# Weight tiles of the projections placed 64, 128 and 256 bytes past multiples of 2 KB in SBUF

## The chip, the cores and the metric

The kernel runs on one core of a Trainium2 chip. The metric is the device time of one execution in microseconds. The kernel before takes 1646.32 us, the median of three runs (1645.86 to 1648.91). All input and output is float32.

## The reference

One decoder layer over 1024 tokens of width 1024. The part that the change touches is the token mixer: one combined input projection of the normalised residual, two convolution branches, and their output projections.

```python
def token_mixer(h, w_in, conv_a_w, w_out_a, conv_b_w, conv_b_b, ln_b_g, ln_b_b, w_out_b, b_gate, w_o):
    proj = h @ w_in                                    # (1024 x 1024) @ (1024 x 7168)
    a_b, a_c, a_x, c_val, c_gate, gates = jnp.split(proj, cuts, axis=-1)
    y_a = (a_b * causal_dwconv(a_c * a_x, conv_a_w)) @ w_out_a
    u = c_val * jax.nn.sigmoid(c_gate)
    u = causal_dwconv(u, conv_b_w) + conv_b_b
    u = jax.nn.silu(layernorm(u, ln_b_g, ln_b_b))
    y_b = u @ w_out_b
    g = jax.nn.sigmoid(gates + b_gate)
    g_a, g_b = jnp.split(g, 2, axis=-1)
    return (g_a * y_a + g_b * y_b) @ w_o

def reference(...):
    h = rmsnorm(x, mix_norm_g[i])
    x = x + token_mixer(h, ...)
    h = rmsnorm(x, ffn_norm_g[i])
    x = x + hierarchical_moe(h, ...)      # top-1 of 4 groups, top-2 of its 8 experts
    hp = rmsnorm(x, ple_norm_g[i])
    x = x + jax.nn.sigmoid(hp @ w_ple_gate[i]) * (p[i] @ w_ple_proj[i])
    return rmsnorm(x, final_norm_g)
```

## The kernel before

**Products.** The projections keep float32 accuracy with three products of split operands in the type float32r: each operand is a high part (the value cast to float32r) and a low part (value minus high part), and a product is high by high, high by low and low by high. In a projection the weights are the stationary operand (128 x 128, loaded by a LDWEIGHTS of its own before each matmul) and the activations the moving one (128 x 512).

**A projection.** `proj` (L165) makes 128 output channels for all 1024 tokens. `wchunk` (L149) brings 128 columns of a weight matrix by one DMA on SP's queue into a raw tile (three buffers) and splits it: ScalarE writes the high part `wh` (L95), VectorE the low part `wl` (L96). `wh` and `wl` are rings of two buffers each in the pool `wring`. `proj_half` (L159) then issues, for one half of the tokens, 24 matmuls (L162): for each of 8 slices k of the contraction wh, wh, wl. So a projection is 48 matmuls, 32 of them with `wh` and 16 with `wl`. There are 72 projections: 56 column blocks of w_in, 8 of w_out_a and 8 of w_out_b, 3456 matmuls in all.

**Stages.** In stage s0 the rows are normalised, transposed and split into the tiles `a0` to `a7`; stage s1 (L227) makes five projections for each of 8 channel blocks, while VectorE runs the 31-tap convolution (L254); stage s2 (L314) makes the gates, both output projections and the layer norm. Then follow the product with w_o (L422), in which activations are stationary and the weights moving, the routing, the experts (L833, L860, plain float32 operands), and the last product with the gate weights (L1207 and L1274, again float32r, activations stationary). The instruction order of the first stages is set by the tile framework's scheduler, that of the later ones is written by hand.

**Addresses.** What matters here is where a tile begins in each partition of SBUF, modulo 2 KB. The pool of constants is padded (L134), so that the tiles `a0` to `a7` and `b0` to `b7`, of 8 KB each, begin at multiples of 2 KB; a moving operand is a run of 2 KB of such a tile, beginning at a multiple of 2 KB. In `wring` stand `vecs` (224 bytes), `cw` (1088) and a pad of 736, which make 2048 together; behind them lie the two buffers of `wh` and the two of `wl`, of 4096 bytes each. So all four begin at a multiple of 2 KB, and slice k of the weights at 512 k bytes behind one. The last product's operands and those of the product with w_o lie in the same way: the stationary ones at steps of 512 bytes from a multiple of 2 KB, the moving ones at a multiple of 2 KB (in L1274 some at 1 KB behind one). Behind `wring` lie the working tiles of the stages s1 and s2.

Of the kernel before, what the change touches and what calls it, by code (L numbers as in the profile page):

```python
# [10 lines left out]
F32 = mybir.dt.float32  # L11
F32R = mybir.dt.float32r
# [10 lines left out]
D = 1024  # L23
NT = 8
KT = 8
# [38 lines left out]
def layer_kernel(ctx: ExitStack, tc: tile.TileContext, A, out, dbg=None):  # L64
# [15 lines left out]
    def tpsum():  # L80
        return psum.tile([128, 512], F32, name="tp", bufs=2)
# [4 lines left out]
    def flat(t):  # L86
        return t.rearrange("p a b -> p (a b)")
# [6 lines left out]
    def split(h, l, src):  # L94
        nc.scalar.activation(h, src, AF.Copy)  # L95
        nc.vector.tensor_tensor(l, src, h.bitcast(F32), op=OP.subtract)  # L96

    def rstd_of(dst, ms):

        nc.gpsimd.tensor_scalar(dst, ms, EPS, None, op0=OP.add)  # L100
        nc.gpsimd.tensor_tensor(dst, dst, mhalf[:, :dst.shape[1]], op=OP.pow)
# [17 lines left out]
    def vec(i, k):  # L119
        return vecs[:, i * 8 + k:i * 8 + k + 1]  # L120
# [18 lines left out]
    wring = front.enter_context(tc.tile_pool(name="wring", bufs=2))  # L139
# [9 lines left out]
    def wchunk(src, c0, load_only=False):  # L149
        raw = wrawp.tile([128, KT, 128], F32, name="wraw")  # L150
        nc.sync.dma_start(raw, src[:, c0:c0 + 128].rearrange("(k p) n -> p k n", p=128))
        wh = wring.tile([128, KT, 128], F32R, name="wh")
        wl = wring.tile([128, KT, 128], F32R, name="wl")
        if load_only:
            return wh, wl, raw
        split(wh, wl, raw)
        return wh, wl
# [7 lines left out]
    def proj(src, c0, act):  # L165
        w = wchunk(src, c0)
        ps = mpsum()
        for hf in range(2):
            proj_half(w, ps, act, hf)
        return flat(ps)  # L170

    with tc.tile_pool(name="s0", bufs=1, side="right") as s0:
# [6 lines left out]
        for tb in range(NT):  # L179
            if tb == 4:  # L180
                first = [wchunk(w_in, (4 - i) * D, load_only=True) for i in range(2)]
            xt = s0.tile([128, D], F32, name=f"xt{tb}")
            nc.sync.dma_start(xt, A["x"][0, tb * 128:(tb + 1) * 128, :])
            xs.append(xt)
            for n, i, m in small[2 * tb:2 * tb + 2]:
                nc.sync.dma_start(vrow[i * 8:(i + m) * 8, :], A[n][0].rearrange("(k p) -> k p", p=128))
# [38 lines left out]


    with tc.tile_pool(name="s1", bufs=2) as s1:  # L227
        for cb in range(8):
            pg = proj(w_in, 4 * D + cb * 128, hT) if cb else flat(fps[0])
            sg = s1.tile([128, T], F32, name="tmp", bufs=2)  # L230
            nc.scalar.activation(sg, pg, AF.Sigmoid)
            pv = proj(w_in, 3 * D + cb * 128, hT) if cb else flat(fps[1])
            u = s1.tile([128, KB - 1 + T], F32, name="u")
            nc.gpsimd.memset(u[:, :KB - 1], 0.0)
            nc.vector.tensor_tensor(u[:, KB - 1:], pv, sg, op=OP.mult)
            acc = s1.tile([128, T], F32, name="acc")
            nc.scalar.activation(acc, u[:, :T], AF.Identity, scale=cw[:, cb, 0:1], bias=vec(V_CB, cb))  # L237
            pc = proj(w_in, D + cb * 128, hT)
            cx = s1.tile([128, T], F32, name="tmp", bufs=2)
            nc.scalar.activation(cx, pc, AF.Copy)  # L240
            px = proj(w_in, 2 * D + cb * 128, hT)
            m = s1.tile([128, 32 + T], F32, name="m", bufs=1)[:, :2 + T]
            nc.gpsimd.memset(m[:, :2], 0.0)
            nc.vector.tensor_tensor(m[:, 2:], px, cx, op=OP.mult)
            c3 = s1.tile([128, T], F32, name="c3", bufs=1)
            nc.scalar.activation(c3, m[:, :T], AF.Copy, scale=cw[:, cb, KB:KB + 1])
            for t in (1, 2):
                nc.vector.scalar_tensor_tensor(c3, m[:, t:t + T], cw[:, cb, KB + t:KB + t + 1], c3,
                                               op0=OP.mult, op1=OP.add)
            pb = proj(w_in, cb * 128, hT)  # L250
            nc.vector.tensor_tensor(c3, pb, c3, op=OP.mult)
            split(Y[0][cb], Y[1][cb], c3)
            for t in range(1, KB):
                nc.vector.scalar_tensor_tensor(acc, u[:, t:t + T], cw[:, cb, t:t + 1], acc,  # L254
                                               op0=OP.mult, op1=OP.add)
            nc.gpsimd.dma_start(u_dram[cb], acc)
# [57 lines left out]


    with tc.tile_pool(name="s2", bufs=2) as s2:
        def gate(c0, vi, ob):
            p = proj(w_in, c0 + ob * 128, hT)
            g = s2.tile([128, T], F32, name="g")
            nc.scalar.activation(g, p, AF.Sigmoid, bias=vec(vi, ob))  # L320
            return g

        def token_stat(acc, name):
            tp = tpsum()
            for tb in range(NT):
                nc.tensor.matmul(tp[:, tb:tb + 1], acc[:, tb * 128:(tb + 1) * 128], ones_col, start=True, stop=True)
            st = s2.tile([128, 32], F32, name=name, bufs=1)[:, :8]
            nc.vector.tensor_scalar(st, tp[:, :8], 1.0 / D, None, op0=OP.mult)
            return st

        def token_bcast(st, name):
            b = s2.tile([128, T], F32, name=name, bufs=1)
            for h in range(2):
                tp = tpsum()
                for j in range(4):
                    nc.tensor.transpose(tp[:, j * 128:(j + 1) * 128],
                                        st[:, h * 4 + j:h * 4 + j + 1].to_broadcast([128, 128]), ident)
                nc.scalar.activation(b[:, h * 512:(h + 1) * 512], tp, AF.Copy)
            return b

        def u_tile(cb):
            ut = s2.tile([128, T], F32, name="ut", bufs=2)
            nc.scalar.dma_start(ut, u_dram[cb])
            return ut

        def branch_a(ob):
            g = gate(5 * D, V_GA, ob)
            pa = proj(A["w_out_a"][0], ob * 128, Y)
            ma = s2.tile([128, T], F32, name="ma")
            nc.vector.tensor_tensor(ma, pa, g, op=OP.mult)  # L350
            nc.gpsimd.dma_start(mixa_dram[ob], ma)

        stat = s2.tile([128, T], F32, name="stat", bufs=1)
        for ob in range(4):
            branch_a(ob)
        for cb in range(0, 8):
            ut = u_tile(cb)
            if cb == 0:
                nc.scalar.activation(stat, ut, AF.Copy)
            else:  # L360
                nc.vector.tensor_tensor(stat, stat, ut, op=OP.add)
        mub = token_bcast(token_stat(stat, "mu"), "mub")
        for ob in range(4, 8):
            branch_a(ob)
        for cb in range(8):
            ut = u_tile(cb)
            nc.vector.tensor_tensor(ut, ut, mub, op=OP.subtract)
            if cb == 0:
                nc.scalar.activation(stat, ut, AF.Square)
            else:  # L370
                nc.scalar.activation(ut, ut, AF.Square)
                nc.vector.tensor_tensor(stat, stat, ut, op=OP.add)
        rs = token_stat(stat, "var")
        rstd_of(rs, rs)
        rsb = token_bcast(rs, "rsb")
        for ob in range(8):
            g = gate(6 * D, V_GB, ob)
            nc.gpsimd.dma_start(gb_dram[ob], g)
        S = Y
        for cb in range(8):  # L380
            ut = u_tile(cb)
            nc.vector.tensor_tensor(ut, ut, mub, op=OP.subtract)
            nc.vector.tensor_tensor(ut, ut, rsb, op=OP.mult)
            nc.scalar.activation(ut, ut, AF.Silu, scale=vec(V_LG, cb), bias=vec(V_LB, cb))
            split(S[0][cb], S[1][cb], ut)
        M = [a.rearrange("p (i k t) -> p i k t", i=2, k=KT) for a in bufA]
        for ob in range(8):
            pb = proj(A["w_out_b"][0], ob * 128, S)
            ma = s2.tile([128, T], F32, name="ma")
            nc.scalar.dma_start(ma, mixa_dram[ob])  # L390
            g = s2.tile([128, T], F32, name="g")
            nc.scalar.dma_start(g, gb_dram[ob])
            nc.vector.tensor_tensor(g, pb, g, op=OP.mult)
            nc.vector.tensor_tensor(ma, ma, g, op=OP.add)
            for tb in range(NT):
                split(M[tb][:, 0, ob], M[tb][:, 1, ob], ma[:, tb * 128:(tb + 1) * 128])
# [306 lines left out]
    n = []  # L703
# [611 lines left out]
```

## Time and profile before

| | |
|---|---|
| median of three runs | 1646.32 us |
| the profiled execution, its own time | 1647.99 us |
| its span, first to last instruction | 1646.2 us |
| mean granted TensorE clock, share of 2.4 GHz | 0.983 |
| TensorE matmuls busy | 1561.0 us, 95% |
| VectorE busy | 814.4 us, 49% |
| ScalarE busy | 351.3 us, 21% |
| matmuls of L162 | 3456 |

The profile gives for a matmul the time from its start to its modelled end, and matmuls overlap: the mean duration of one at L162 is some 390 ns, but the next starts long before that. The rate of a stream is read from the starts: the count in a stretch in which TensorE never rests, or the difference of two starts in the order of time. An instruction is counted in a window when any part of it lies in it.

### The profile page before, as it was taken

How to read it: one execution, taken by the hardware profiler on the slowest of the kernel's cores; microseconds unless marked ns; L12 is line 12 of the kernel's file. 1: busy time of each engine (PE TensorE's matmuls, PEld its weight loads, DVE VectorE, ACT ScalarE, POOL GpSimd, SP SyncE). 2: the span in 40 equal slices, each digit the busy share in tenths (PEclk: the TensorE clock that was granted, in tenths of full speed). 3: DMA queues.
4: the chain of work that ended last, by engine and by line, in shares of the span. 5: the costliest groups of instructions: out<-in, count | busy, mean ns of one | idle time of the engine just before them, and what ended most of it. 6: DMA issues, size and time to landing. Idle time of an engine off the chain costs nothing. (4 is left out here: it accounts for less than half of the span.)

```text
span 1646.2 us, 20527 instructions
## 1 busy us (share of the span) xinstructions
PE 1561.0 (95%) x8112; PEld 1068.9 (65%) x8112; DVE 814.4 (49%) x1113; ACT 351.3 (21%) x533; POOL 170.9 (10%) x318
## 2 busy tenths in 40 slices
PE   6999999999999999999999798999999999798898
PEld 4888888888888888888878642344444443343586
DVE  4899999999983432515554521111111212411575
ACT  4222212221121223632321210010100101010443
POOL 2300000000000001000022221111110101010131
PEclk9999999999999999999999988999999999899999
DMA  5221122212225333534365699999994989799741
GB/s 170 62 65 57 46 64 64 65 39 65 64 97 177 122 117 106 163 122 147 128 243 192 237 356 396 411 400 409 363 406 178 382 351 352 292 349 413 295 166 52
DMA packets 190669, 336.76 MB, mean 205 GB/s; under 512 B 10182, under 2 KB 85022, under 8 KB 190560
## 3 DMA queue, kind: packets, MB, share of 16 engines
q1 hardware_dynamic: 174080, 284.13, 47.5%
q0 software_dynamic: 10576, 29.96, 5.0%
q10 hardware_dynamic: 5904, 21.24, 4.0%
q8 instruction: 66, 1.08, 0.3%
q14 instruction: 43, 0.35, 0.1%
HBM read 302.67 MB, written 35.11 MB: 205 GB/s over the span
## 5 line engine op out<-in xcount | busy, mean ns | idle before, releaser
L162 PE MATMUL mm<-a,wh 128*128 128x512 f32 x1792 | 556.1, 391 | 0.9 <-ACT a L213 0.9
L162 PEld LDWEIGHTS mm<-a,wh 128*128 128x128 f32 x1792 | 336.9, 188 | 71.3 <-ACT a L213 1.5
L162 PE MATMUL mm<-a,wl 128*128 128x512 f32 x896 | 349.4, 390 | 0.0
L254 DVE SCALAR_TENSOR_TENSOR acc<-u,cw,acc 128x1024 f32<-128x1024 f32 x240 | 307.9, 1283 | 7.9 <-ACT acc L237 1.9
L162 PEld LDWEIGHTS mm<-a,wl 128*128 128x128 f32 x896 | 168.5, 188 | 34.4
L95 ACT ACTIVATE wh<-wraw 128x1024 fp32r<-128x1024 f32 x72 | 76.4, 1061 | 494.1 <-PE mm L162 422.7
L162 PE MATMUL mm<-b,wh 128*128 128x512 f32 x512 | 157.6, 389 | 0.0
L833 PE MATMUL p<-a,xts 128*32 128x256 f32 (+2 forms) x600 | 138.9, 520 | 8.4 <-DMA a<-in_w_exp_up_dram 5.1
L96 DVE TENSOR_TENSOR wl<-wraw,wh 128x1024 fp32r<-128x1024 f32 x72 | 87.7, 1218 | 72.9 <-ACT wh L95 72.8
L871 DVE COPY ys<-p 32x256 f32<-32x256 f32 (+2 forms) x60 | 31.3, 521 | 185.5 <-ACT ys L871 126.9
L833 PE MATMUL p<-b,xts 128*32 128x256 f32 (+2 forms) x528 | 109.6, 460 | 2.5 <-DMA b<-in_w_exp_up_dram 2.5
L162 PEld LDWEIGHTS mm<-b,wh 128*128 128x128 f32 x512 | 96.1, 188 | 19.9
L162 PE MATMUL mm<-b,wl 128*128 128x512 f32 x256 | 99.6, 389 | 0.0
L422 PE MATMUL mm<-b,a 128*128 128x512 f32 x384 | 95.8, 399 | 1.3 <-DVE b L96 1.3
L871 ACT COPY ys<-p 32x256 f32<-32x256 f32 (+2 forms) x60 | 26.6, 443 | 329.6 <-PE p L860 329.3
L833 PEld LDWEIGHTS p<-a,xts 128*32 128x32 f32 (+2 forms) x600 | 44.5, 136 | 78.7 <-issue 64.0
L838 DVE TENSOR_TENSOR hid<-p,hid 64x256 f32<-64x256 f32 (+2 forms) x41 | 22.7, 560 | 119.4 <-ACT hid L837 62.6
L422 PEld LDWEIGHTS mm<-b,a 128*128 128x128 f32 x384 | 69.6, 188 | 16.3 <-DVE b L96 2.1
L847 DVE COPY hT<-h 128x128 f32<-128x128 f32 (+2 forms) x41 | 17.3, 421 | 113.8 <-PE h L846 113.8
L833 PEld LDWEIGHTS p<-b,xts 128*32 128x32 f32 (+2 forms) x528 | 39.5, 133 | 43.6 <-issue 34.7
L699 POOL DMA_INDIRECT c<-h_dram,idx x39 | 37.8, 969 | 285.4 <-PE x L797 242.1
L860 PE MATMUL p<-a,hT 128*32 128x256 f32 (+2 forms) x440 | 67.4, 463 | 0.0
(322 smaller groups left out, 1551.2 us busy)
## 6 DMA issues: line engine op xcount, KB each, us to landing
a<-in_w_exp_down_dram SPq DMA_DIRECT2D x32, 1024.0 KB, 13.3
a<-in_w_exp_gate_dram SPq DMA_DIRECT2D x31, 1024.0 KB
b<-in_w_exp_up_dram SPq DMA_DIRECT2D x30, 1024.0 KB, 12.9
wraw<-in_w_in_dram SPq DMA_DIRECT2D x56, 512.0 KB, 3.6
b<-in_w_exp_down_dram SPq DMA_DIRECT2D x28, 1024.0 KB, 12.5
a<-in_w_exp_up_dram SPq DMA_DIRECT2D x27, 1024.0 KB, 13.1
b<-in_w_exp_gate_dram SPq DMA_DIRECT2D x24, 1024.0 KB
ut<-u_dram ACTq DMA_DIRECT2D x24, 512.0 KB, 4.6
```

What stands on the lines that cost most here:

```text
L95: nc.scalar.activation(h, src, AF.Copy)
L96: nc.vector.tensor_tensor(l, src, h.bitcast(F32), op=OP.subtract)
L162: nc.tensor.matmul(ps[:, hf], w[wi][:, k], act[ai][k][:, hf * 512:(hf + 1) * 512], start=(k == 0 and i == 0), stop=(k == KT - 1 and i == 2))
L254: nc.vector.scalar_tensor_tensor(acc, u[:, t:t + T], cw[:, cb, t:t + 1], acc, op0=OP.mult, op1=OP.add)
L422: nc.tensor.matmul(ps[-1][:, hf], act(a, k), w(b, k)[:, hf * 512:(hf + 1) * 512], start=(k == 0 and i == 0), stop=(k == nk - 1 and i == 2))
L699: return nc.gpsimd.indirect_dma_start(out=xg, out_offset=None, in_=h2_dram, in_offset=bass.IndirectOffsetOnAxis(ap=ix[:, 0:1], axis=0), bo ...
L833: nc.tensor.matmul(self.gu[j][p:p + r], self.x[:, k], w[:, i:i + self.gu[0].shape[1]], start=(k == 0), stop=(k == KT - 1))
L838: nc.vector.tensor_tensor(self.h, self.gu[1], self.h, op=OP.mult)
L847: nc.vector.tensor_copy(self.hT[:, :4], tp.rearrange("p (f t) -> p f t", f=4))
L860: nc.tensor.matmul(d, self.hT[:, f // 2 + f % 2 * 2 if r == 32 else f], w[:, c * n:(c + 1) * n], start=(f == 0), stop=(f == 3))
L871: (nc.scalar.copy if c < len(self.d) // 2 else nc.vector.tensor_copy)(self.y[:, c * n:(c + 1) * n], d)
```

## The change

The tile `wh` is made 16 elements (64 bytes) longer and `wl` 32 elements (128 bytes); the added elements are not used. With two buffers each, the four begin at 0 (`wh`, first buffer), 64 (`wh`, second), 128 (`wl`, first) and 256 bytes (`wl`, second) behind a multiple of 2 KB. These are 384 bytes more, and a pad of 1664 bytes at the head of s1 and of s2 makes them up to 2048: the working tiles of both stages move by exactly 2 KB and keep their places modulo 2 KB. All other tiles stay where they were. The instructions of every engine, their order, their shapes and what each waits for are the same as before; only addresses differ.

```diff
     def wchunk(src, c0, load_only=False):
         raw = wrawp.tile([128, KT, 128], F32, name="wraw")
         nc.sync.dma_start(raw, src[:, c0:c0 + 128].rearrange("(k p) n -> p k n", p=128))
-        wh = wring.tile([128, KT, 128], F32R, name="wh")
-        wl = wring.tile([128, KT, 128], F32R, name="wl")
+
+        wh = wring.tile([128, D + 16], F32R, name="wh")[:, :D].rearrange("p (k n) -> p k n", k=KT)
+        wl = wring.tile([128, D + 32], F32R, name="wl")[:, :D].rearrange("p (k n) -> p k n", k=KT)
         if load_only:
             return wh, wl, raw
         split(wh, wl, raw)
...
     with tc.tile_pool(name="s1", bufs=2) as s1:
+        s1.tile([128, 416], F32, name="pads", bufs=1)
...
     with tc.tile_pool(name="s2", bufs=2) as s2:
+        s2.tile([128, 416], F32, name="pads", bufs=1)
```

## Rows read from the trace of the kernel before

**Rows 1.** Four stretches of the projection stages: busy time of each engine in us, with the number of instructions in brackets, then the granted TensorE clock, the DMA share and GB/s.

```profile
200.00:400.00 200.00, 200.00 (x884) 165.63 (x883) 184.62 (x151) 38.75 (x37) 2.96 (x11) 1.00 0.20 61
400.00:500.00 100.00, 100.00 (x443) 82.80 (x442) 85.48 (x70) 20.50 (x20) 1.70 (x4) 1.00 0.27 85
620.00:700.00 80.00, 80.00 (x366) 66.39 (x365) 35.00 (x31) 41.58 (x39) 5.90 (x8) 1.00 0.43 138
700.00:800.00 100.00, 100.00 (x443) 82.83 (x442) 36.20 (x64) 28.32 (x58) 2.13 (x4) 1.00 0.41 132
```

The columns are: stretch, its length, PE, PEld, DVE, ACT, POOL, clock, DMA share, GB/s.

**Rows 2.** The page's costliest groups: the matmuls of the projections, the splits of their weights and the convolution. Columns: line, engine, operation, out<-in with shapes, count | busy us, mean ns of one | idle us before, and what ended it.

```profile
L162 PE MATMUL mm<-a,wh 128*128 128x512 f32 x1792 | 556.1, 391 | 0.9 <-ACT a L213 0.9
...
L162 PE MATMUL mm<-a,wl 128*128 128x512 f32 x896 | 349.4, 390 | 0.0
L254 DVE SCALAR_TENSOR_TENSOR acc<-u,cw,acc 128x1024 f32<-128x1024 f32 x240 | 307.9, 1283 | 7.9 <-ACT acc L237 1.9
...
L95 ACT ACTIVATE wh<-wraw 128x1024 fp32r<-128x1024 f32 x72 | 76.4, 1061 | 494.1 <-PE mm L162 422.7
L162 PE MATMUL mm<-b,wh 128*128 128x512 f32 x512 | 157.6, 389 | 0.0
...
L96 DVE TENSOR_TENSOR wl<-wraw,wh 128x1024 fp32r<-128x1024 f32 x72 | 87.7, 1218 | 72.9 <-ACT wh L95 72.8
...
L162 PE MATMUL mm<-b,wl 128*128 128x512 f32 x256 | 99.6, 389 | 0.0
```

**Rows 3.** The matmuls in order of time from 200 us, equal neighbours merged. Columns: start us, us from the first start to the last modelled end, engine, line, operation, out<-in, form, count.

```profile
199.87 0.39 PE L162 MATMUL mm<-a,wl 128*128 128x512 f32 x1
200.10 0.62 PE L162 MATMUL mm<-a,wh 128*128 128x512 f32 x2
200.55 0.39 PE L162 MATMUL mm<-a,wl 128*128 128x512 f32 x1
200.78 0.62 PE L162 MATMUL mm<-a,wh 128*128 128x512 f32 x2
201.23 0.39 PE L162 MATMUL mm<-a,wl 128*128 128x512 f32 x1
201.46 0.62 PE L162 MATMUL mm<-a,wh 128*128 128x512 f32 x2
201.91 0.39 PE L162 MATMUL mm<-a,wl 128*128 128x512 f32 x1
...
202.59 0.39 PE L162 MATMUL mm<-a,wl 128*128 128x512 f32 x1
...
203.27 0.39 PE L162 MATMUL mm<-a,wl 128*128 128x512 f32 x1
...
203.95 0.39 PE L162 MATMUL mm<-a,wl 128*128 128x512 f32 x1
...
204.63 0.39 PE L162 MATMUL mm<-a,wl 128*128 128x512 f32 x1
...
205.31 0.39 PE L162 MATMUL mm<-a,wl 128*128 128x512 f32 x1
```

**Rows 4.** The chain that ended last, in order of time, in the last product: start us, us, engine, what, line, count. The 48 at L1207 are 128 x 512; the 48 at L1274 are 24 of 128 x 512 and 24 of 128 x 256; the 24 of `h` at L1274 are 128 x 256.

```profile
1599.36 10.90 PE p L1207 x48
...
1627.01 8.31 PE p L1274 x48
1635.32 2.89 PE h L1274 x24
```

**Rows 5.** Matmuls of the experts in order of time, 128 x 512 on plain float32 operands, each with a weight load of its own; columns as in rows 3.

```profile
1250.15 13.90 PE L860 MATMUL p<-b,hT 128*128 128x512 f32 x32
```

**Rows 6.** Matmuls of the product with w_o right after two small matmuls of the routing have broken into the stream; columns as in rows 3.

```profile
903.08 0.28 PE L580 MATMUL tp<-payf,at 128*64 128x2 f32 x2
903.28 3.26 PE L422 MATMUL mm<-b,a 128*128 128x512 f32 x13
```

**Rows 7.** A weight load in the stream of rows 3, from the same view with TensorE's loads (PEld) in it; columns as there.

```profile
201.24 0.41 PEld L162 LDWEIGHTS mm<-a,wh 128*128 128x128 f32 x2
```

## The prediction

> **What bounds the kernel now.** I read the table of stretches first, because a change of addresses can only act where an engine reads or writes the moved tiles and these live in the stages s0 to s2. In four stretches of these TensorE is busy for the whole of each, 480 of 480 us, at a granted clock of 1.00, that is 2.4 GHz [rows 1]. Next the costliest groups: the 3456 matmuls of L162 stand in four groups, and TensorE sat idle 0.9 us before them in all [rows 2]. So these stages are as long as TensorE's matmuls follow each other, and nothing else sets their length. The splits that write the moved tiles are off the path: ScalarE's writes of wh wait 422.7 us in total for matmuls to give a buffer back, and VectorE's writes of wl wait for ScalarE [rows 2].
>
> **The rate of the stream.** From 200 to 400 us 884 matmuls are counted; one lasts 0.39 us and is counted from its start, so the window takes in starts over 200.39 us, and one follows the other by 200.39 / 884 = 226.7 ns [rows 1, 3]. At 2.4 GHz 512 columns take 213.3 ns, so each matmul has 13.4 ns that no column explains. Is it a fixed price or a share? The last product gives the answer with the same kind of operands: 48 of 512 columns in 10.90 us are 227.1 ns each, 24 of 256 columns in 2.89 us are 120.4 ns each, against 213.3 and 106.7 ns for the columns [rows 4]. The extra is 13.8 and 13.7 ns: a fixed price for each pair of weight load and matmul. Multiplied by the 3456 matmuls of L162 it is some 46 us of the kernel, and this is all that an address could give back.
>
> **The change part by part.** No instruction is added, removed or moved, and no wait. What remains are three terms.
>
> First, matmuls whose weights lie elsewhere. In a ring of two each buffer serves 36 of the 72 projections. The first buffer of wh stays at its place and with it 36 x 32 = 1152 matmuls. The second buffer of wh has 1152, the two of wl 576 each: 2304 matmuls get another offset between weights and moving operand. Their price at the new offset isn't in the trace, so I bound it. The lowest: the experts' matmuls of the same shape on plain float32 follow each other by (13.90 - 0.59) / 31 = 429 ns, with 0.59 us for the last one's duration, which is two passes of 214.7 ns [rows 5]; with the pair at that, 12.0 ns go, and 2304 x 12.0 = 27.6 us are won. The highest: after a break in the stream, 13 matmuls in the product with w_o take (3.26 - 0.39) / 12 = 239 ns each, the slowest unstalled run of that shape that I found, and this contains what the break itself cost [rows 6]; at that price 2304 x 12.5 = 28.8 us are lost.
>
> I take neither, but zero, for two reasons from rows. Slice k of the weights begins at 512 k bytes, so before the change the weight reads already begin at four different places modulo 2 KB, while the moving operand always begins at a multiple of 2 KB. If the meeting of equal places cost anything, slices 0 and 4 would be slower than 1, 2 and 3. The wl matmuls stand one per slice, and the differences of their starts are 0.68 us eight times in a row, 3 x 226.7 ns [rows 3]: all slices cost the same to within the 10 ns of the rows, about 3 ns for one matmul. And the reads do not stand still at their start: one weight read walks through 512 bytes, a moving read through 2 KB, in the same time. An offset of 64 to 256 bytes shifts when the two pass equal places, not how often they do. What these rows cannot exclude is an effect of the bits below 512 bytes at the start alone, because every start before is a multiple of 512. This is what keeps both ends in the range.
>
> The two-pass rows of the experts do not decide it. They have the same layout and almost no extra, but they take twice as long over the same bytes, so a collision could hide there.
>
> The fixed price is the same for all slices and in a product with quite other tiles [rows 3, 4]. The Trainium skill, in "TensorE: Matmul & The Clock Gate", section "Step-by-step: what each phase is for", says that TensorE has two independent read ports into SBUF, and that loading the next weights takes no read bandwidth from the running matmul. By that rule the sum of this term is 0 at any offset, as by the rows; 27.6 us would be won only if the rule failed.
>
> Second, the splits. ScalarE's write of wh takes 1.06 us and VectorE's subtraction 1.22 us, once per projection of 48 x 226.7 ns = 10.9 us [rows 2]. I know of no row that prices them at another offset; none is written across a different number of bytes. The cover: a channel block of s1 is five projections, 54.4 us, of which VectorE is busy 184.62 / 200, that is 50.2 us [rows 1]. The 4.2 us left are 0.84 us for each of five subtractions; they would have to grow from 1.22 to 2.06 us before TensorE waited. Value 0; each 0.1 us by which a subtraction grew beyond that would cost 40 x 0.1 = 4 us over the eight blocks. The cover holds in the other direction too: were 160 of the 240 matmuls of a block 12.0 ns faster, the block would be 52.5 us, still more than VectorE's 50.2.
>
> Third, the working tiles of s1 and s2, moved by 2 KB: their places modulo 2 KB are the same, and so are their waits. 0.
>
> Sum: 0 us. The profiled execution has a span of 1646.2 us and 1.8 us around it, 1647.99 us; it lies 1.7 us above the median of the runs, and since the sum is 0 the forecast is that median, 1646.3 us.
>
> **The rivals.** One: the reads do collide, and the offset resolves it. For it speaks that a fixed 13.7 ns stands beside each weight load [rows 4], and that a pass of 214.7 ns exists on this chip [rows 5]. Against it stand the equal slices [rows 3]. Its time is 1646.3 - 27.6 = 1618.7 us in full; where only some of the moved buffers gain, half of that, about 1632 us.
>
> A rule of the skill would make the same case: "TensorE: Matmul & The Clock Gate", section "Back-to-back issue gap", gives N / 2.4 + 2.5 ns, 215.8 ns for 512 columns. By it 10.9 ns of each matmul are to be had, an estimate of 25.1 us on 2304 matmuls, or 1621 us. The trace does not agree with that figure for these operands: it has 226.7 ns in steady state.
>
> Two, on the other side: the aligned start is the good one. The mechanism: the weight load of a wh pair starts at 201.24 us, the wl matmul that streams beside it at 201.23 us [rows 3, 7]: the two reads set out together, and with both at a multiple of 512 bytes the two reads may keep a fixed step that makes them miss each other, and a start 64 to 256 bytes off would break that step. For it speaks that the spacing is not one constant: after a break the same matmuls are slower for a while [rows 6]. Against it that the two reads cover unlike lengths in the same time. It decides from the first projection with a moved tile on; from 1.4 ns per moved matmul, 3.3 us in all, it shows as slower. Its price runs up to 28.8 us (1675 us); a mean of 3.5 ns, about a quarter of that end, gives 8 us, 1654 us.
>
> Three: the change doesn't do what it says. One third of the matmuls keep their offset, so whatever the offset does, only two thirds can show it; this is in the counts above and no case of its own.
>
> **How the numbers follow.** What can be told from no change is about 0.2%, 3.3 us. No effect: 0.68. Rival one: 0.17, of which 0.07 for the full gain and 0.10 for a part. Rival two, with the splits' case in it: 0.15. The range reaches from 1632 us, half of the full gain, to 1656 us, some 4 ns per moved matmul; what lies outside I put at 0.07 and a little below and 0.07 above. The case of no effect has a range of its own of 1643 to 1649.6 us.
>
> **What would show it.** Right: from 200 to 400 us again 884 matmuls, give or take two, wl starts 0.68 us apart in every projection, TensorE without idle time at L162, the writes at L95 and L96 at 1.06 and 1.22 us. Rival one shows as more matmuls in that stretch, up to 916 (two thirds at 214.7 ns and one third at 226.7, a mean of 218.7), with wl steps that differ from projection to projection as the buffers alternate. Rival two shows as fewer, 875 at a mean loss of 3.5 ns on two thirds. The prediction is wrong if the spacing in s1 differs between the two buffers, or if the time differs by over 3.3 us with the same spacing, which would mean a place that I did not name.

## The result and the profile after

The changed kernel takes 1662.14 us (median of four runs, 1658.54 to 1665.55) against 1647.54 us before (median of four): a ratio of 1.009 with a 95% interval of 1.0072 to 1.0109. It is slower by some 15 us; the forecast was no change, and its range ended at 1656 us.

The profiled execution has a span of 1663.8 us, 17.6 us more than before. The same stretches as in [rows 1], with the same columns:

```profile
200.00:400.00 200.00, 200.00 (x866) 162.97 (x865) 181.07 (x148) 38.03 (x36) 2.96 (x11) 1.00 0.19 58
400.00:500.00 100.00, 100.00 (x434) 81.44 (x433) 89.38 (x73) 18.06 (x17) 1.17 (x4) 1.00 0.21 66
620.00:700.00 80.00, 80.00 (x360) 65.36 (x359) 28.94 (x25) 35.83 (x33) 5.38 (x7) 1.00 0.38 120
700.00:800.00 100.00, 100.00 (x434) 81.50 (x433) 35.22 (x56) 32.62 (x56) 2.65 (x5) 1.00 0.42 136
```

TensorE is busy for the whole of each stretch and at full clock, as before. It only does less: 866 matmuls in the first 200 us and not 884, so one follows the other by 200.39 / 866 = 231.4 ns, where it was 226.7. VectorE's busy time falls with it (181.07 for 184.62 us), because it is fed more slowly.

How much of the loss is there? The view of one line gives the first and last start of its instructions. Of the kernel before, the first and last matmuls of the projections:

```profile
L162 PE MATMUL mm<-a,wh x1792: 387/389/796, 17.2 to 730.9; 128*128 128x512 f32 x200
...
L162 PE MATMUL mm<-b,wl x256: 388/389/390, 476.0 to 818.2; 128*128 128x512 f32 x128
```

and of the changed kernel (the line numbers are one higher):

```profile
L163 PE MATMUL mm<-a,wh x1792: 387/393/796, 17.8 to 745.2; 128*128 128x512 f32 x200
...
L163 PE MATMUL mm<-b,wl x256: 389/394/398, 485.4 to 834.2; 128*128 128x512 f32 x128
```

The projections last 834.2 - 17.8 = 816.4 us, before 818.2 - 17.2 = 801.0 us: 15.4 of the 17.6 us are in them, the whole size of the measured loss. The splits, which write the moved tiles, are as fast as in [rows 2], and the longer wait of ScalarE for TensorE is slack:

```profile
L95 ACT ACTIVATE wh<-wraw 128x1024 fp32r<-128x1024 f32 x72 | 76.4, 1061 | 515.8 <-PE mm L163 442.5
...
L96 DVE TENSOR_TENSOR wl<-wraw,wh 128x1024 fp32r<-128x1024 f32 x72 | 87.7, 1219 | 76.6 <-ACT wh L95 76.4
```

In order of time, the wl matmuls of one projection with the second buffers (wh at 64, wl at 256 bytes) and then of one with the first (wh at 0, wl at 128); columns as in [rows 3]:

```profile
200.93 0.39 PE L163 MATMUL mm<-a,wl 128*128 128x512 f32 x1
...
206.48 0.39 PE L163 MATMUL mm<-a,wl 128*128 128x512 f32 x1
...
208.56 0.40 PE L163 MATMUL mm<-a,wl 128*128 128x512 f32 x1
...
212.03 0.40 PE L163 MATMUL mm<-a,wl 128*128 128x512 f32 x1
```

Eight steps of three matmuls take 5.55 us with the second buffers and five take 3.47 us with the first: 694 ns for three in both, where [rows 3] has 680. So every projection is slower by the same 13 to 14 ns for three matmuls, although a third of the matmuls kept their weights' place.

Which of the three steps grew? The answer is worked out from the starts of projections 4 to 46 in the trace, from the fifth triple of each on. With the first buffers, the second wh matmul follows the first after 226.7 ns, as before; the wl matmul follows after 232.5 ns, and the next wh after 234.2. With the second buffers the steps are 225.8, 235.8 and 231.6 ns. So the loss sits at the steps into and out of the wl matmul, and the step between two wh matmuls costs nothing, even in the second buffers, where wh itself lies at 64 bytes.

### The profile page after: what moved, and what is told of

It is laid out like the page before. It is cut to its first block, busy times and chain, and to the rows that moved or that the text cites. A ratio compares the mean times of both kernels' runs of the same rounds, so it can differ in the third digit from the quotient of the medians.

```text
span 1663.8 us, 20527 instructions
## 1 busy us (share of the span) xinstructions
PE 1579.8 (95%) x8112; PEld 1072.5 (64%) x8112; DVE 815.0 (49%) x1113; ACT 351.4 (21%) x533; POOL 171.1 (10%) x318
## 5 line engine op out<-in xcount | busy, mean ns | idle before, releaser
L163 PE MATMUL mm<-a,wh 128*128 128x512 f32 x1792 | 562.6, 395 | 0.9 <-ACT a L214 0.9
L163 PE MATMUL mm<-a,wl 128*128 128x512 f32 x896 | 354.9, 396 | 0.0
L95 ACT ACTIVATE wh<-wraw 128x1024 fp32r<-128x1024 f32 x72 | 76.4, 1061 | 515.8 <-PE mm L163 442.5
L96 DVE TENSOR_TENSOR wl<-wraw,wh 128x1024 fp32r<-128x1024 f32 x72 | 87.7, 1219 | 76.6 <-ACT wh L95 76.4
L163 PEld LDWEIGHTS mm<-b,wh 128*128 128x128 f32 x512 | 96.4, 188 | 23.3
## 6 DMA issues: line engine op xcount, KB each, us to landing
a<-in_w_exp_down_dram SPq DMA_DIRECT2D x32, 1024.0 KB, 13.4
```

The lines of the kernel that those rows point to most:

```text
L163: nc.tensor.matmul(ps[:, hf], w[wi][:, k], act[ai][k][:, hf * 512:(hf + 1) * 512], start=(k == 0 and i == 0), stop=(k == KT - 1 and i == 2))
```

## The experiments

The unit below is the time of three successive matmuls of a projection (wh, wh, wl), 680 ns before; 72 projections have 1152 such triples. Three theories stood at first. A: a pair of load and matmul is dearer when the weights lie at another distance from the moving operand. B: what costs is that successive loads begin at different places, as wh and wl do. C: what costs is that the two buffers of a ring differ.

**All four tiles at 64 bytes.** The weight tiles get room to be placed by a function, on bases that are multiples of 1 KB; the other runs with `OFFSETS` (in elements of 4 bytes, for wh and wl of projection n) use the same lines.

```diff
+def OFFSETS(n):
+    return 16, 16
...
-        wh = wring.tile([128, KT, 128], F32R, name="wh")
-        wl = wring.tile([128, KT, 128], F32R, name="wl")
+        oh, ol = OFFSETS(turns[0])
+        turns[0] += 1
+        wh = wring.tile([128, D + 256], F32R, name="wh")[:, oh:oh + D].rearrange("p (k n) -> p k n", k=KT)
+        wl = wring.tile([128, D + 256], F32R, name="wl")[:, ol:ol + D].rearrange("p (k n) -> p k n", k=KT)
```

> All four weight tiles begin 64 bytes past a multiple of 512 bytes; the moving operand stays at multiples of 2 KB. Theory A (distance: a pair of load and matmul is dearer when the weights lie at another place than the moving operand): slower, since 64 bytes is one of the offsets of the changed kernel; three matmuls (wh, wh, wl) take about 693 ns as there, and the kernel about 1663 us. Theory B (change: what costs is that successive weight loads begin at different places modulo 512 bytes, as wh and wl do in the changed kernel; the distance to the moving operand costs nothing): no change, 680 ns for three matmuls, 1647 us.

1671.89 us, ratio 1.0146 (1.0113 to 1.0179). The first stretch, columns as in [rows 1]:

```profile
200.00:400.00 200.00, 200.00 (x859) 161.56 (x858) 179.42 (x146) 38.07 (x36) 2.95 (x11) 1.00 0.19 58
```

200.39 / 859 = 233.3 ns for one, 700 ns for three: dearer than the changed kernel, with all four tiles alike. B and C fall as the whole cause, A stands, with a larger price than it had named (20 and not 13 ns; 1152 x 20 = 23.0 us, measured 23.3). Here all three steps are 233.3 ns, the one between two wh matmuls too.

**The low part alone at 128 bytes.**

```diff
+def OFFSETS(n):
+    return 0, 32
```

> One part of the change alone: both buffers of wl begin 128 bytes past a multiple of 512 bytes, both of wh at a multiple. Theory A: only the wl matmuls can pay, in all projections; if 128 bytes cost what they cost in the changed kernel's first buffers, 693 ns for three matmuls, about 1663 us. Theory B: wh and wl differ in every projection, so the full price although only a third of the matmuls have moved: 693 ns for three, about 1663 us. Theory C (what costs is that the two buffers of a ring lie at different places, so that one projection differs from the next): no change, 680 ns and 1647 us.

1663.15 us, ratio 1.0095 (1.0061 to 1.0129), with 867 matmuls in the first stretch:

```profile
200.00:400.00 200.00, 200.00 (x867) 163.82 (x866) 181.16 (x148) 38.06 (x36) 2.96 (x11) 1.00 0.20 60
```

231.1 ns for one, 693 for three: one matmul in three has moved, and the loss is that of the whole change. C falls again. From the starts, the step into the wl matmul is 232.5 ns, the one out of it, to a wh that has not moved, 234.2, and the one between two wh matmuls 226.7.

**Two maps.** Each projection has a pair of its own. In the first map the 35 pairs follow each other and come again in reverse order.

```diff
+BYTES = (
+    (0, 0), (16, 16), (32, 32), (64, 64), (128, 128), (256, 256), (448, 448),
+    (0, 16), (0, 32), (0, 48), (0, 64), (0, 96), (0, 128), (0, 192),
+    (0, 256), (0, 320), (0, 384), (0, 448), (0, 480), (16, 0), (32, 0),
+    (64, 0), (128, 0), (256, 0), (384, 0), (64, 128), (64, 192), (128, 64),
+    (256, 128), (128, 256), (64, 256), (0, 512), (0, 1024), (512, 0), (0, 544),
+)
+def OFFSETS(n):
+    if n < 2:
+        return 0, 0
+    oh, ol = BYTES[n - 2 if n < 37 else 71 - n]
+    return oh // 4, ol // 4
```

> A map: each of 70 projections has its own pair of offsets for wh and wl (35 pairs, each twice, the second time in reverse order). Read is what three matmuls (wh, wh, wl) take within a projection. Theory A: pairs of equal offsets (16 to 448 bytes) are as dear as (0, same offset), about 693 ns; (0, 0) 680 ns. Theory B: equal offsets 680 ns at any offset; unequal ones about 693 ns, and the same for (0, o) as for (o, 0); differences of 512 and 1024 bytes 680 ns, (0, 544) as (0, 32). Either theory leaves open whether the price grows with the difference or steps up at some size; a flat one would be 693 ns from 16 to 480 bytes.

In the second every pair is entered from a projection at (0, 0), and `BYTES` is another list of 35 pairs.

```diff
+def OFFSETS(n):
+    if n < 3 or n % 2 == 0:
+        return 0, 0
+    oh, ol = BYTES[(n - 3) // 2]
+    return oh // 4, ol // 4
```

> A second map, in which every second projection has both weight tiles at 0, so that each pair of offsets is met from the same state. If the distance modulo 256 bytes decides: (256, 256), (512, 512) 680 ns for three matmuls; (272, 272) as (16, 16), (320, 320) as (64, 64), (32, 288) as (32, 32), (64, 320) as (64, 64), (128, 384) as (128, 128). The pairs with 16 bytes or less, entered from 680 ns, are expected at 680 ns; if one stands below 680 ns, the price of 13 ns that the kernel before pays at each pair of load and matmul can be lowered by an address, and otherwise it can't by this means.

The reading is the step from one wl matmul to the next. Four projections of the second map, ten steps apart each: (32, 32), then (0, 0), then (256, 256), then (320, 320).

```profile
173.56 0.40 PE L182 MATMUL mm<-a,wl 128*128 128x512 f32 x1
...
180.56 0.40 PE L182 MATMUL mm<-a,wl 128*128 128x512 f32 x1
...
182.63 0.39 PE L182 MATMUL mm<-a,wl 128*128 128x512 f32 x1
...
189.44 0.39 PE L182 MATMUL mm<-a,wl 128*128 128x512 f32 x1
...
591.37 0.39 PE L182 MATMUL mm<-b,wl 128*128 128x512 f32 x1
...
598.17 0.39 PE L182 MATMUL mm<-b,wl 128*128 128x512 f32 x1
...
635.63 0.40 PE L182 MATMUL mm<-b,wl 128*128 128x512 f32 x1
...
642.63 0.40 PE L182 MATMUL mm<-b,wl 128*128 128x512 f32 x1
```

These are 700, 681, 680 and 700 ns a step. The table has the same reading of most of the pairs, as the mean of a projection's sixteen triples, worked out from all the starts in the two traces (two values: both maps' or both passes' readings):

```
wh and wl both at o bytes:   4: 697   8: 692   12: 680   16: 680 or 700   24: 693   32: 700
                            48: 700  64: 700   96: 703  128: 697  160: 700  192: 687  224: 700
                           240: 680 248: 700  252: 680  256: 680  272: 680  320: 700  512: 680
wl alone (0, o):            16: 680, 696  32: 699, 700  64: 693, 693  128: 694, 693  192: 693, 693
                           256: 680, 681 384: 694, 695 448: 693, 693  512: 680  544: 699  1024: 680
wh alone (o, 0):            16: 680 to 699  32: 696, 696  64: 700, 700  128: 700, 700
                           256: 680 (683 where other matmuls broke in)  384: 700, 701  512: 681
```

Three things follow. First, the price repeats with 256 bytes: (320, 320) is (64, 64), (0, 544) is (0, 32), and multiples of 256 cost nothing. Theory A holds in this form. It does not hold as a price that each matmul pays by its own distance: wl alone at 64 bytes makes 693 ns, wh alone 700, and both together 700. Nor was either expectation met in full: A had equal offsets as dear as one tile moved alone, and the second map had the pairs at 4 and 8 bytes at 680 ns, where they stand at 692 to 700. Second, nothing is below 680 ns: of the offsets tried none gives back the 13.4 ns that each pair pays before the change. Third, at 16 bytes the outcome depends on what came before. In the first map (16, 16) stands once behind (0, 0) and once behind (32, 32):

```profile
62.44 0.39 PE L182 MATMUL mm<-a,wl 128*128 128x512 f32 x1
...
69.24 0.39 PE L182 MATMUL mm<-a,wl 128*128 128x512 f32 x1
...
810.55 0.40 PE L182 MATMUL mm<-b,wl 128*128 128x512 f32 x1
...
817.55 0.40 PE L182 MATMUL mm<-b,wl 128*128 128x512 f32 x1
```

6.80 us for ten steps the first time and 7.00 us the second, from the same offsets. These two differ in the ring's buffer and in the moving tile as well. A pair that doesn't is (16, 0), in the second buffers and with the moving tiles `a` both times, in the first map behind (0, 480) and in the second behind (0, 0):

```profile
260.99 0.39 PE L182 MATMUL mm<-a,wl 128*128 128x512 f32 x1
...
267.99 0.39 PE L182 MATMUL mm<-a,wl 128*128 128x512 f32 x1
...
434.65 0.39 PE L182 MATMUL mm<-a,wl 128*128 128x512 f32 x1
...
441.45 0.39 PE L182 MATMUL mm<-a,wl 128*128 128x512 f32 x1
```

Again 7.00 and 6.80 us. The changed kernel's own second pair, (64, 256), does it too: it takes 694 ns there, entered from (0, 128), and 700 ns both times in the first map, the second time entered from (0, 512):

```profile
482.29 0.40 PE L182 MATMUL mm<-b,wl 128*128 128x512 f32 x1
...
489.29 0.40 PE L182 MATMUL mm<-b,wl 128*128 128x512 f32 x1
```

So it is no fixed charge on an address, and the map's entry for a pair is a reading from one state. The offsets 12, 240 and 252 were met only once alike for both tiles, from the fast state. In the changed kernel the starts show that after a few triples the three steps repeat to the end of a projection (with the second buffers 226, 236 and 232 ns). It looks as if the two reads of TensorE fell into one pattern or another and stayed in it, which the runs suggest and don't show.

**The order of the products.** On the changed kernel's addresses:

```diff
-            for i, (wi, ai) in enumerate(((0, 0), (0, 1), (1, 0))):
+            for i, (wi, ai) in enumerate(PASSES[::-1] if k % 2 else PASSES):
```

> The changed kernel's addresses, but every second slice of the contraction takes its three products in reverse order (wl, wh, wh after wh, wh, wl), so that wl loads stand in pairs and the change between wh and wl happens twice in six matmuls and not four times. Theory A: the same pairs of addresses, so the same price, 693 ns for three and about 1662 us. Theory B: half the changes, half the price: about 687 ns for three and 1655 us.

1667.12 us, ratio 1.0119 (1.0085 to 1.0152), 862 matmuls in the first stretch, 697 ns for three. Fewer changes between wh and wl made it dearer, not cheaper, which is against B; and the steps between two equal tiles, wh and wh or wl and wl, are slow here as well, 231 to 235 ns from the starts. It isn't A's unchanged 693 either; the price depends on the order in which the offsets follow each other.

**Which of the two operands.** Theory A leaves open whether the distance counts (R), the weights' own place (W), or the place of each operand (V). First everything behind the constants is moved by 64 bytes:

```diff
-    const.tile([128, 104], F32, name="pad")
+    const.tile([128, 120], F32, name="pad")
```

> The pad of the constants is 64 bytes longer, so that the moving operands, the weight tiles and all tiles behind them move by 64 bytes together; the distance between weights and moving operand is that of the kernel before. Theory R (what counts is the distance from the start of the moving operand to that of the weights, modulo 256 bytes): no change, 680 ns for three matmuls, 1647 us. Theory W (the weights themselves must begin at multiples of 256 bytes, the moving operand may lie anywhere): slow, as with the weights alone at 64 bytes, 700 ns and about 1671 us. Theory V (each of the two operands must begin at such a multiple): slow too, 700 ns or more.

Then the moving operand without the weight tiles (the raw tiles that are split go with it), by the same line and

```diff
-    wring.tile([128, 184], F32, name="padw", bufs=1)
+    wring.tile([128, 168], F32, name="padw", bufs=1)
```

> The moving operands begin 64 bytes past a multiple of 2 KB, the weight tiles at a multiple of 2 KB as before. Theory R: slow, about 695 to 700 ns for three matmuls, since the distance is now 192 modulo 256; 1665 to 1671 us. Theory W: no change, 680 ns and 1647 us. Theory V: slow. R and V are told apart by the kernel with everything moved together.

The first stretch with everything moved:

```profile
200.00:400.00 200.00, 200.00 (x884) 165.62 (x883) 184.67 (x151) 39.12 (x37) 2.97 (x11) 1.00 0.19 60
```

and with the moving operand moved against the weight tiles:

```profile
200.00:400.00 200.00, 200.00 (x875) 164.09 (x875) 182.80 (x148) 38.02 (x36) 2.97 (x11) 1.00 0.20 61
```

884 matmuls, 680 ns for three: weights at 64 bytes cost nothing when the moving operand lies there too, so W and V fall. 875 matmuls, 687 ns: the weight tiles haven't moved and the rate falls, to the very 687 ns that the map has for a distance of 192 bytes (0 - 64 is 192 modulo 256). R holds; that run's expectation of 695 to 700 ns was a guess ahead of that entry of the map. The times of the whole kernels, 1658.23 us (ratio 1.0058, 1.0036 to 1.0079) and 1666.53 us (1.0107, 1.0078 to 1.0137), are some 10 us above what the projections explain; the last section takes that up.

**A stagger in steps of 256 bytes.**

```diff
+def OFFSETS(n):
+    return ((0, 128), (64, 192))[n % 2]
```

> The weight tiles are staggered as in the changed kernel, each buffer at a place of its own, but in steps of 256 bytes (0 and 512, 256 and 768 past a multiple of 1 KB) and not of 64 and 128. If a stagger as such cost something, about 1662 us; if only distances that are no multiple of 256 bytes do, no change: 680 ns for three matmuls and 1647 us.

1650.09 us, ratio 1.0006 (0.9992 to 1.0020), and the first stretch as before the change:

```profile
200.00:400.00 200.00, 200.00 (x884) 165.60 (x883) 184.67 (x150) 38.38 (x37) 2.97 (x11) 1.00 0.20 61
```

A stagger as such is harmless; this one also moves the tiles of s1 and s2 by 4 KB, and nothing came of that.

**A forecast from the map.** One line of the kernel before is moved to another place:

```diff
-    wring.tile([128, 184], F32, name="padw", bufs=1)
...
     with tc.tile_pool(name="s1", bufs=2) as s1:
+        s1.tile([128, 184], F32, name="pads", bufs=1)
...
     with tc.tile_pool(name="s2", bufs=2) as s2:
+        s2.tile([128, 184], F32, name="pads", bufs=1)
```

> The pad of 736 bytes ahead of the weight tiles is taken out and put ahead of the working tiles of s1 and s2: all four weight tiles begin 1312 bytes past a multiple of 2 KB, which is 32 modulo 256, and the moving operand at 0. By the two maps the pair (32, 32) takes 699.5 ns for three matmuls, 19.5 ns more than 680; 1152 such triples make 22.5 us, so 1670.5 us. If what counts were a stagger of the four tiles among themselves, they have none here: 1648 us.

1670.51 us, ratio 1.0154 (1.0132 to 1.0176), with 858 matmuls in the first stretch:

```profile
200.00:400.00 200.00, 200.00 (x858) 160.99 (x858) 179.41 (x146) 38.10 (x36) 2.96 (x11) 1.00 0.19 58
```

The map's entry for (32, 32) gives the time of the whole kernel: 23.6 us lost, where the entry makes 22.5; that the total agrees to 0.01 us is luck. The run also shows what the pad of 736 bytes is worth in the kernel before: some 23 us.

No run beat the kernel before: its weights already lie at the cheapest distance that was found.

## Why the prediction was wrong

**What bounds the kernel.** Right: TensorE sets the length of these stages, busy for the whole of the four stretches in both kernels, and 15.4 of the 17.6 us were lost there.

**The fixed price.** Its size was right (13.4 ns beside the columns), and so was the use made of [rows 4]. Of "all that an address could give back", no offset tried gave back anything.

**The first term** is the step that failed: it was set at 0 and is 15.4 us. Both reasons given for zero were wrong. The first, that slices at 512 k bytes all cost the same [rows 3], rested on rows that could not speak: 0, 512, 1024 and 1536 are all 0 modulo 256, so the four places were one place. The prediction said itself that bits below 512 were open, and then gave that too little weight. The second, "an offset of 64 to 256 bytes shifts when the two pass equal places, not how often they do", is refuted by the maps: the rate changes with the offset. Its premise, that the two reads take the same time, isn't in the rows either: 165.63 us for 883 loads are 188 ns for one [rows 1], and the matmuls follow each other after 226.7. The bounds held: the dearest whole kernel lost 23.6 us (1670.51 against 1646.94 us), within the 28.8 us taken from [rows 6].

**Whom it touches.** The count of 2304 moved matmuls was wrong as a measure, and so was "only two thirds can show it". Every projection slows alike, and within it the steps into and out of the wl matmul: with wl alone moved, the wh matmul behind it is late too (234.2 ns), and in the changed kernel the wh matmuls that moved are on time among themselves (225.8 ns). So the price isn't that of the moved weights alone; it depends on what follows what in the stream. The prediction's own signs of being wrong, a spacing that differs between the buffers or another time at the same spacing, left out what came: another spacing, the same in both.

**The rule on the two reads.** Weighed in the prediction, the Trainium skill ("TensorE: Matmul & The Clock Gate", section "Step-by-step: what each phase is for") has loading the next weights take nothing from the running matmul. These runs do not agree: with everything else equal the matmul rate follows the distance between the starts of the two operands, 226.7 to 233.3 ns. The Trainium skill's formula for the gap (same page, section "Back-to-back issue gap"), 215.8 ns for 512 columns, stands there for an isolated matmul and not, as the prediction used it, for a stream of pairs of load and matmul; it was reached at no offset tried.

**The splits and the working tiles.** Right: 1061 and 1219 ns, no cover was needed, and the working tiles, moved by 2 KB here and by 4 KB in the run with steps of 256 bytes, cost nothing that shows.

**Rival two** had the sign and the place, and of its mechanism the first half: equal starts are the good ones. That the reads set out together and keep a step is not shown, and its bounds were wrong: a start 256 bytes off, which it counted among the bad ones, costs nothing, and starts that are all 64 bytes off cost nothing either. It was mis-sized: 3.5 ns on 2304 matmuls, 8 us, against 15.4 / 3456 = 4.5 ns on all of them. Its own range reached the result; the chance of 0.15 for it was too small, and the range of the whole ended 6 us too early. Its sign in the trace was the one that it named, fewer matmuls in the stretch (866; it said 875).

**Rival one** fell: no offset tried made a projection faster. Its pass of 214.7 ns was half of the 429 ns of [rows 5]; that these are two passes is shown by no run.

What stays open is what in the memory has the period of 256 bytes, why some distances (12, 240, 252) cost nothing and their neighbours do, what puts the stream into one pattern or the other, and whether the slow matmuls after a break [rows 6] are the same effect. No run tried these.

## What to carry to other kernels

In a stream of float32r matmuls that each load their weights, keep the distance between the start of the weights and the start of the moving operand at a multiple of 256 bytes, for every weight tile in the stream; a stray tile of a few hundred bytes ahead of either cost some 3% of the stream's rate here (233.3 ns for 226.7). When a trace shows no difference between several addresses, look first at what they have in common: equal costs at 0, 512, 1024 and 1536 say nothing of 64. A map with one setting per loop turn gives dozens of such readings from one execution; enter each setting from more than one neighbour, since the one before can decide the reading.

## What the runs showed of the hardware

That the rate of a matmul stream depends on the distance of its two operands modulo 256 bytes, and that the stream can stay fast or slow at the same offsets (680 or 700 ns for three matmuls at (16, 0)), was not expected.

Nor was the loss of the kernel whose tiles had all moved by 64 bytes. Its projections ran at 680 ns, so it was lost elsewhere. The experts' stage, from the first of its transposes to the last of its matmuls, before and with everything moved by 64 bytes (columns as in [rows 1]):

```profile
947.40:1526.00 578.60, 535.98 (x3430) 227.74 (x3434) 115.90 (x230) 55.49 (x115) 76.03 (x82) 0.97 0.95 362
```

```profile
944.50:1530.00 585.50, 540.58 (x3430) 228.01 (x3434) 115.87 (x230) 55.59 (x115) 76.23 (x82) 0.96 0.97 358
```

It takes 6.9 us longer, with the DMA engines busier (0.97 for 0.95) and moving less (358 for 362 GB/s). Not all of that is the tiles: the stage of the kernel with steps of 256 bytes, whose target tiles had not moved, and that of the kernel with the moving operand at 64 bytes, whose target tiles had, are

```profile
948.00:1529.00 581.00, 540.66 (x3434) 228.69 (x3434) 115.87 (x230) 55.59 (x115) 76.22 (x82) 0.96 0.95 361
```

```profile
954.70:1540.00 585.30, 539.08 (x3432) 228.74 (x3434) 115.87 (x230) 55.59 (x115) 76.22 (x82) 0.96 0.97 357
```

Measured in all twelve traces, the stage lasts 579 to 581 us in the ten with the tiles `a` and `b` at multiples of 256 bytes and some 586 us in the two with them at 64. The same tiles moved by 256 bytes tell whether that goes:

```diff
-    const.tile([128, 104], F32, name="pad")
+    const.tile([128, 168], F32, name="pad")
```

> As the run that moved everything by 64 bytes, but by 256. That run had its projections at 680 ns for three matmuls and yet lost some 10 us, 7 of them in the experts' stage, where the DMA queues brought at most 398 GB/s in a slice and not 413. Theory F (the transfers into tiles that begin 64 bytes off are slower): at 256 bytes this goes, if 256 suffices as a boundary; 680 ns, 1648 us, slices of 413 GB/s again. Theory G (it is the distance between these tiles and the constants, which stay where they are, or to the ends of memory): still about 1657 us.

1648.79 us, ratio 1.0014 (0.9999 to 1.0028): it goes. The GB/s line of the page's 40 slices, for 64 bytes and then for 256:

```profile
GB/s 170 62 65 64 39 64 64 65 50 53 64 120 162 115 115 129 141 126 153 133 259 183 237 360 381 394 384 391 388 388 209 364 364 350 300 345 397 298 166 52
```

```profile
GB/s 170 62 63 54 51 64 64 64 40 64 64 93 177 120 122 101 168 119 146 132 244 191 237 359 397 410 401 396 354 406 178 379 370 352 294 346 413 293 166 52
```

The fastest slice has 397 GB/s with tiles 64 bytes off and 413 GB/s at 256, as theory F has it. In a stage whose DMA engines are busy for 0.95 of the time, an offset of 64 bytes in the target tiles was worth 4 to 7 us in the profiled executions. Of everything moved by 64 bytes that execution, at 1652.28 us, was the fastest of its kernel's runs; where the other runs lost the rest of their 10 us isn't shown. Which boundary between 64 and 256 bytes suffices was not tried.
